# Transposing each normalized row block once in the first pass of a split-precision Strassen product

## The chip, the cores and the metric

The kernel runs on one core of a Trainium2 chip, in one launch. The metric is the device time of the program in microseconds (us). Of the kernel before the change, three runs gave 2653.09, 2655.56 and 2656.48 us, a median of 2655.56.

## The reference, cut to what matters

Two layers work on x of 2048 rows by 1024. The change lies in the first layer's first product, h @ w_in:

```python
h = rms_norm(x, a_norm_g)            # x * rsqrt(mean(x*x) + 1e-6) * g
u, v, z = split(h @ w_in, 3)         # w_in: 1024 x 6144
u = gelu(u)
v = layer_norm(gelu(v), a_ln_g, a_ln_b)
mixed = W_s applied to v in groups of 128 rows, + b_s
x = x + (u * mixed * silu(z)) @ w_out
```

The second layer (chunked band attention and its products) follows and is not touched.

## The kernel before

All data are float32. A float32 factor is split into a high and a low part (type fp32r), and a product is made of three matmuls, high by high, high by low and low by high (`mm3`, lines L111 to L113). The high part is a cast on ACT (L434), the low part a subtraction on DVE (L437), both in `split`.

The product h @ w_in is done by Strassen's scheme. h is cut into 16 row blocks of 128; pair j (0 to 7) is made of block 2j, held in the tile `ha` j, and block 2j+1, held in `hb` j. Each block has two halves of 512 columns: a11, a12 in `ha`, b1, b2 in `hb`. Seven combinations of these four halves are the stationary factors, called S_1 to S_7: S_1 = a11, S_2 = a12, S_4 = b2, S_5 = b1 + b2, S_6 = S_5 - a11, S_7 = a11 - b1 (kept in the tile `h21`), S_3 = a12 - S_6. The additions and subtractions are made by POOL: L734 (h21), L735 (b1 += b2), L736 (a11 becomes S_6), L753 (a12 becomes S_3). The weights are combined likewise: `rw` is a raw weight tile, `ch` a sum of such tiles (POOL, L445), and `T` the split factor.

The columns of w_in are cut into passes n = 0 to 5. A pass has seven phases in the order 1, 2, 6, 5, 7, 4, 3 (`PH`), each with a step for each of the eight pairs. In the phases 1 and 2 of n = 0, a step serves the pass n = 1 too and has two products; every other step has one. A product is twelve matmuls into one PSUM bank (tag "mm", four banks), which is evicted by ACT in phase 1 (L574) and by DVE elsewhere (L570); c, x and y are the accumulators.

A factor must have the inner dimension on the partitions, so each combination is transposed on PE, four 128 x 128 transposes (L611) into a PSUM tile `t0` of one bank (tag "t0", four banks). `s_split` does this in the pass n = 0: it transposes, splits into a tile S (six buffers), and one step later stores the tile to DRAM (`hsd`, L614, on SP's queue, ordered behind the latest eviction by `paced`). Every later use loads it from `hsd` (L602).

`run_steps` writes the program's order: at step s first the list `events[s]`, then the products and evictions of the step, then `prep` of step s + 3, which makes or loads that step's S, then the list `ts[s]`. `prep0` is the `prep` of n = 0: it makes S_1, S_2, S_6 and S_3 and loads the others. S_4, S_5 and S_7 are made ahead: `block_c` makes S_4 and issues the three POOL operations, `block_d` makes S_5, and S_7 is made in phase 5.

`block_norm` returns the four functions that normalize a block: the load of x (L697, SP), the Square with row sums (L703, ACT), the power -0.5 (L709 on DVE, L710 on POOL), the scaling by the row factor and g (L714, DVE). `norm_at` puts them into `ts` and `events`; blocks 0 and 2 (the pairs 0 and 1) are normalized before the first step. A scheduler then orders the instructions of each engine, so an engine's order need not be the order written.

Of the kernel before, what the change touches and what calls it, by code (L numbers as in the profile page):

```python
# [9 lines left out]
F32 = mybir.dt.float32  # L10
# [7 lines left out]
P = 128  # L18
S = 2048
# [14 lines left out]
def trunk_kernel(  # L34
# [19 lines left out]
    nc = tc.nc  # L54
# [26 lines left out]
    ident = cst.tile([P, P], F32, name="ident")  # L81
# [26 lines left out]
    mm, tpose = nc.tensor.matmul, nc.tensor.transpose  # L108
# [46 lines left out]
    def block(t, b):  # L155
        xt = xf[t, b]
        half = [
            banks[0].tile([P, 4, P], F32, tag="t4", name=f"tr_b{t}_{b}_{h}", bufs=4)
            for h in range(2)
        ]  # L160
        for k in range(KD):
            ins = tpose(half[k // 4][:, k % 4, :], xt[:, k * P : (k + 1) * P], ident[:])
            if k == 0:
                on_tick(ins)
        x3 = xt[:].rearrange("p (k c) -> p k c", k=KD)
        for h in range(2):
            ks = slice(h * 4, h * 4 + 4)
            nc.scalar.copy(x3[:, ks, :], half[h][:])
        nc.sync.dma_start(xtd[t][:, b, :], xt[:])
# [214 lines left out]
    with ExitStack() as actx:  # L384
# [26 lines left out]
        def s_tile(name):  # L411
            return ca.tile([P, 2, 4, P], F32R, tag="S", name=name, bufs=6)
# [10 lines left out]
        def in_order(key, ins):  # L423
            if key in last:
                behind(ins, last[key])
            last[key] = ins.ins.name

        def paced(ins):

            if "evict" in last:  # L430
                behind(ins, last["evict"])

        def split(hi, lo, src, key=None):
            ins = nc.scalar.copy(hi, src)  # L434
            if key:
                in_order(key, ins)
            nc.vector.tensor_tensor(lo, src, hi.bitcast(F32), op=sub)  # L437
            return ins
# [158 lines left out]
        def s_views(t):  # L597
            return [(t[:, 0, k, :], t[:, 1, k, :]) for k in range(4)]

        def s_load(ph, j, n):  # L600
            t = s_tile(f"S{n}_{ph}_{j}")
            nc.sync.dma_start(  # L602
                t[:].rearrange("p a k c -> p a (k c)").bitcast(F32), hsd[ph, j][:]
            )
            return s_views(t)

        def s_split(ph, j, rows):

            pt = ptp[0].tile([P, 4, P], F32, tag="t0", name=f"t0_{ph}_{j}", bufs=4)
            for k in range(4):  # L610
                tpose(pt[:, k, :], rows[:, k * P : k * P + P], ident[:])  # L611
            t = s_tile(f"S0_{ph}_{j}")
            split(t[:, 0], t[:, 1], pt[:], "S")
            later(1, lambda: paced(nc.sync.dma_start(  # L614
                hsd[ph, j][:], t[:].rearrange("p a k c -> p a (k c)").bitcast(F32)
            )))
            return s_views(t)
# [5 lines left out]
        def later(steps, f_):  # L623
            late.append((now[0] + steps, f_))
# [62 lines left out]
        ptp = [ptx.enter_context(tc.tile_pool(name="pt0", bufs=1, space=PSUM))]  # L687
        gab = p0.tile([P, D], F32, name="gab")
        ha = {}
        h21 = {}  # L690

        def block_norm(blk, t):

            r = sm.tile([P, 1], F32, tag="rr", name=f"ra{blk}", bufs=4)

            def load():
                nc.sync.dma_start(t, x[blk * P : (blk + 1) * P, :])  # L697
                if blk == 0:
                    nc.sync.dma_start(gab[:], a_norm_g.partition_broadcast(P))

            def square():
                jk = ca.tile([P, D], BF16, tag="acc", name=f"jk{blk}", bufs=25)
                ins = nc.scalar.activation(  # L703
                    jk[:], t, AF.Square, scale=1.0 / 32, accum_out=r[:]
                )
                last["square"] = ins.ins.name

            def power():
                nc.vector.tensor_scalar(r[:], r[:], EPS, None, op0=add)  # L709
                ins = nc.gpsimd.tensor_tensor(r[:], r[:], mhalf[:], op=ALU.pow)  # L710
                last["power"] = ins.ins.name

            def scale():
                nc.vector.scalar_tensor_tensor(t, t, r[:], gab[:], op0=mul, op1=mul)  # L714

            return load, square, power, scale

        def block_a(j):
            h = ha[j] = p0.tile([P, D], F32, tag="ha", name=f"ha{j}", bufs=8)
# [3 lines left out]

        def block_b(j):
            h = hb[j] = p0.tile([P, D], F32, tag="hb", name=f"hb{j}", bufs=3)
            return block_norm(2 * j + 1, h[:])

        def block_c(j):

            h = hb[j]  # L730
            s3 = h21[j] = p0.tile([P, 512], F32, tag="h21", name=f"h21_{j}", bufs=8)
            a11, b1_, b2_ = ha[j][:, 0:512], h[:, 0:512], h[:, 512:1024]
            s_split(4, j, b2_)
            behind(nc.gpsimd.tensor_tensor(s3[:], a11, b1_, op=sub), last["power"])  # L734
            nc.gpsimd.tensor_tensor(b1_, b1_, b2_, op=add)  # L735
            nc.gpsimd.tensor_tensor(a11, b1_, a11, op=sub)  # L736
# [7 lines left out]
        def prep0(ph, j):  # L744
            a11, a12 = ha[j][:, 0:512], ha[j][:, 512:1024]
            if ph == 1:
                return s_split(1, j, a11)
            if ph == 2:
                return s_split(2, j, a12)
            if ph == 6:  # L750
                return s_split(6, j, a11)
            if ph == 3:
                nc.gpsimd.tensor_tensor(a12, a12, a11, op=sub)  # L753
                return s_split(3, j, a12)
            return s_load(ph, j, 0)
# [131 lines left out]
        ts = {}  # L887
        events = {}

        def at(s, f_):  # L890
            events.setdefault(s, []).append(f_)

        for n in range(6):
            for ph in PH:
                where = in_t(n, ph)
                s = start.get((n, ph), start[0, ph])
# [18 lines left out]
        def norm_at(load, s, block, j):  # L915
            todo = []

            def first():
                todo.extend(block(j))
                todo.pop(0)()  # L920

            ts.setdefault(load, []).append(first)
            at(s, lambda: todo.pop(0)())
            ts.setdefault(s, []).append(lambda: todo.pop(0)())
            at(s + 1, lambda: todo.pop(0)())

        def first_two():
            for fs in zip(block_a(0), block_a(1)):
                for f_ in fs:
                    f_()  # L930
# [7 lines left out]
        ])  # L938
        at(1, lambda: nc.scalar.mul(bsh[:], bsh[:], 0.5))
        for j in range(NJ):  # L940
            e = j * 7 // 4
            norm_at(e - 1, e, block_b, j)
            at(e + 2, lambda j=j: block_c(j))
            at(e + 4, lambda j=j: block_d(j))
            at(start[0, 5] + j, lambda j=j: s_split(7, j, h21[j]))
# [12 lines left out]
        for n in range(2, 6):  # L958
# [3 lines left out]
            for r, offs in ((0, (5, 9, 13, 17)), (1, (22, 25, 28, 31))):  # L962
                for q, o in enumerate(offs):
# [4 lines left out]
                    if r == 0:  # L968
                        for i in range(2):
                            j = 2 * q + i  # L970
# [308 lines left out]
    with ExitStack() as bctx:  # L1279
# [613 lines left out]
        for t in range(NT):  # L1893
            for p in range(NPAIR):
# [3 lines left out]
                todo = []  # L1898
                if t + 1 == NT and p + 1 == NPAIR:
                    o_early[t - 1, 3] = o_right(t - 1)(3)  # L1900
                    todo = last_open()
                if t == 1 and p < 4:
                    todo = o_sums(p, lambda n: half_tile("C", n, 4), lambda n: half_tile(
                        "S", n, 4, F32R
                    ))
# [90 lines left out]
```

## Time and profile before

| | before |
| --- | --- |
| median of three runs | 2655.56 us |
| span of the profiled execution | 2652.0 us |
| around the span (median less span) | 3.56 us |
| mean granted clock of PE | 0.996 |
| ACT copy x<-P, 128 x 512 (L574) | 596 ns |
| DVE low part S<-t,S, 128 x 512 (L437) | median 682 ns |

No time is given for the profiled execution by itself; its span is 2652.0 us. In a row of the timeline, the first number is the start in us, the second the length in us, and the bracket holds the idle time before it with what ended it. In a row of a group the numbers are the busy time in us and the mean ns of one, then the engine's idle time before these instructions with its releaser. `T<-rw,T` means output T, inputs rw and T; buffer numbers are left out. PE is the matmul unit, PEld its weight loads, PEclk the clock that it was granted. SPq is SP's queue: a DMA instruction there ends when it is issued, not when its data lands.

### The profile page before, as it was taken

How to read it: one execution, taken by the hardware profiler on the slowest of the kernel's cores; microseconds unless marked ns; L12 is line 12 of the kernel's file. 1: busy time of each engine (PE TensorE's matmuls, PEld its weight loads, DVE VectorE, ACT ScalarE, POOL GpSimd, SP SyncE). 2: the span in 40 equal slices, each digit the busy share in tenths (PEclk: the TensorE clock that was granted, in tenths of full speed). 3: DMA queues.
4: the chain of work that ended last, by engine and by line, in shares of the span. 5: the costliest groups of instructions: out<-in, count | busy, mean ns of one | idle time of the engine just before them, and what ended most of it. 6: DMA issues, size and time to landing. Idle time of an engine off the chain costs nothing. (4 is left out here: it accounts for less than half of the span.)

```text
span 2652.0 us, 37980 instructions
## 1 busy us (share of the span) xinstructions
PE 2608.0 (98%) x12960; PEld 2181.4 (82%) x12960; DVE 1885.1 (71%) x2944; ACT 1303.2 (49%) x2303; POOL 897.2 (34%) x874
## 2 busy tenths in 40 slices
PE   8999999999999999999989999999999999999997
PEld 7888888888888888888878878888888888888886
DVE  5655676865767667757767767777778777877677
ACT  5422243442533434343356456666666655666564
POOL 3611334142152322203234434344332232332245
PEclk9999999999999999999999999999999999999999
DMA  7898998989989869967776597778787666875667
GB/s 286 313 344 329 346 370 323 323 323 338 330 302 313 308 233 324 331 206 270 280 251 214 186 280 229 231 245 263 252 270 254 226 204 224 255 230 161 195 224 251
DMA packets 273856, 718.72 MB, mean 271 GB/s; under 512 B 28800, under 2 KB 68736, under 8 KB 273664
## 3 DMA queue, kind: packets, MB, share of 16 engines
q1 hardware_dynamic: 273664, 716.31, 78.4%
q8 instruction: 103, 1.69, 0.3%
q14 instruction: 89, 0.73, 0.1%
HBM read 531.12 MB, written 174.59 MB: 266 GB/s over the span
## 5 line engine op out<-in xcount | busy, mean ns | idle before, releaser
L111 PE MATMUL P<-T,S 128*128 128x512 f32 x1248 | 496.2, 398 | 2.1 <-ACT S L434 2.1
L112 PE MATMUL P<-T,S 128*128 128x512 f32 x1248 | 488.2, 391 | 1.1 <-DVE T L437 1.1
L113 PE MATMUL P<-T,S 128*128 128x512 f32 x1248 | 488.6, 391 | 0.0
L1417 POOL TENSOR_SCALAR pr<-pr,sl 128x640 f32<-128x640 f32 (+4 forms) x256 | 209.7, 819 | 530.4 <-DVE sl L1416 445.2
L111 PE MATMUL pj<-hh_b,wh_b 128*128 128x512 f32 x768 | 320.4, 417 | 0.0
L113 PE MATMUL pj<-hh_b,wl_b 128*128 128x512 f32 x768 | 305.0, 397 | 1.2 <-DVE wl_b L229 1.1
L112 PE MATMUL pj<-hl_b,wh_b 128*128 128x512 f32 x768 | 303.4, 395 | 0.1
L1413 ACT ACTIVATE pr<-pr,nm 128x640 f32<-128x640 f32 (+4 forms) x256 | 195.5, 764 | 188.1 <-DVE nm L1406 186.6
L113 PEld LDWEIGHTS P<-T,S 128*128 128x128 f32 x1248 | 234.9, 188 | 50.5
L111 PEld LDWEIGHTS P<-T,S 128*128 128x128 f32 x1248 | 235.5, 189 | 46.9 <-ACT S L434 2.3
L112 PEld LDWEIGHTS P<-T,S 128*128 128x128 f32 x1248 | 235.6, 189 | 46.1 <-DVE T L437 1.3
L1438 DVE TENSOR_TENSOR pt<-tp,pt 128x640 fp32r<-128x640 f32 (+4 forms) x256 | 188.4, 736 | 43.7 <-ACT pt L1437 41.1
L1406 DVE CUSTOM_DVE_ANT_0 pr<-s,bias 128x640 f32<-128x640 f32 (+4 forms) x256 | 187.9, 734 | 35.7 <-PE s L1398 29.8
L1437 ACT CAST pt<-tp 128x640 fp32r<-128x640 f32 (+4 forms) x256 | 159.0, 621 | 54.0 <-PE tp L1433 49.8
L1433 PE MATMUL tp<-ident,pr 128*128 128x128 f32 x1120 | 166.7, 275 | 8.6 <-DVE pt L1438 7.3
L113 PEld LDWEIGHTS pj<-hh_b,wl_b 128*128 128x128 f32 x768 | 144.7, 188 | 36.4 <-DVE wl_b L229 3.8
L1433 PEld LDWEIGHTS tp<-ident,pr 128*128 128x128 f32 x1120 | 130.7, 140 | 43.3 <-issue 13.7
L111 PEld LDWEIGHTS pj<-hh_b,wh_b 128*128 128x128 f32 x768 | 145.8, 190 | 18.1 <-ACT wh_b L228 1.6
L1458 PEld LDWEIGHTS pv<-pt,V 128*128 128x128 f32 x896 | 143.3, 189 | 20.8 <-DVE pt L1438 3.9
L112 PEld LDWEIGHTS pj<-hl_b,wh_b 128*128 128x128 f32 x768 | 145.8, 190 | 17.1 <-DVE hl_b L186 0.6
L1458 PE MATMUL pv<-pt,V 128*128 128x256 f32 (+3 forms) x896 | 154.5, 320 | 2.2 <-ACT pt L1437 1.1
L229 DVE TENSOR_TENSOR wl_b<-raw_b,wh_b 128x1024 fp32r<-128x1024 f32 x96 | 120.4, 1255 | 28.5 <-ACT wh_b L228 27.8
(294 smaller groups left out, 5725.9 us busy)
## 6 DMA issues: line engine op xcount, KB each, us to landing
S<-hsd SPq DMA_DIRECT2D x288, 512.0 KB, 5.3
rw<-in_w_a SPq DMA_DIRECT2D x108, 512.0 KB, 6.3
A<-ytd SPq DMA_DIRECT2D x72, 512.0 KB, 5.7
raw_b<-wk SPq DMA_DIRECT2D x72, 512.0 KB, 4.3
hsd<-S SPq DMA_DIRECT2D x56, 512.0 KB, 4.9
V<-vhd SPq DMA_DIRECT2D x56, 512.0 KB, 5.4
bias<-reld SPq DMA_DIRECT2D x64, 320.0 KB, 4.2
va<-vd SPq DMA_DIRECT2D x32, 512.0 KB, 5.5
```

The lines of the kernel that those rows point to most:

```text
L111: first = mm(ps, lh, rh, start=first, stop=False)
L112: mm(ps, lh, rl, start=False, stop=False)
L113: mm(ps, ll, rh, start=False, stop=last)
L229: tv(wl[:], raw[:], wh[:].bitcast(F32), op=sub)
L1406: nc.vector.tensor_tensor_reduce(out=pr[:, c0:].rearrange("p (a b) -> p a b", a=nseg), in0=ps[:, :nseg, :w], in1=bias[:, c0:].rearrange("p ...
L1413: nc.scalar.activation(pr[:, c0:], pr[:, c0:], AF.Exp, scale=-1.0, bias=nm[:], accum_out=sl[:])
L1417: nc.gpsimd.tensor_scalar(pr[:, c0:], pr[:, c0:], sl[:], 1.0, op0=ALU.mult, op1=ALU.mult)
L1433: ins = tpose(tp[:, b, :], pr[:, b * P : (b + 1) * P], ident[:])
L1437: nc.scalar.copy(oh, tp[:, b0:5, :].rearrange("p a b -> p (a b)"))
L1438: nc.vector.tensor_tensor(pt[:, 2560 + o + b0 * P : 2560 + o + 640], tp[:, b0:5, :].rearrange("p a b -> p (a b)"), oh.bitcast(F32), op=ALU ...
L1458: mm(po[:, q0 * P : q1 * P], vtl[t, p][:, i, hs], rhs, start=(i == blocks[0] and j == 0), stop=(i == 7 and j == 1),)
```

## The change

The transposes leave `s_split`. `block_norm` gets a fifth function, `turn`: it transposes both halves of a normalized block, eight transposes into two PSUM tiles, which are kept in the table `turned`. `put_back` copies such a tile over the half that it came from, on ACT. From then on `ha` and `hb` hold the transposed halves, and the POOL operations and splits work on these. A B block is put back right behind its turn; an A block in `prep0` of phase 1, behind the split of S_1, which still reads the PSUM tile. All other splits read SBUF. The turn is written one step behind the block's scaling. The B blocks come at e = 2j instead of e = 7j // 4, and their loads two steps ahead of e instead of one.

```diff
         def s_split(ph, j, rows):
-            pt = ptp[0].tile([P, 4, P], F32, tag="t0", name=f"t0_{ph}_{j}", bufs=4)
-            for k in range(4):
-                tpose(pt[:, k, :], rows[:, k * P : k * P + P], ident[:])
             t = s_tile(f"S0_{ph}_{j}")
-            split(t[:, 0], t[:, 1], pt[:], "S")
+            split(t[:, 0], t[:, 1], rows.rearrange("p (k c) -> p k c", k=4), "S")
...
-            return load, square, power, scale
+            def turn():
+                for i in range(2):
+                    pt = ptp[0].tile([P, 512], F32, tag="t0", name=f"t0_{blk}_{i}", bufs=4)
+                    for k in range(4):
+                        c = slice(k * P, k * P + P)
+                        tpose(pt[:, c], t[:, i * 512 + k * P : i * 512 + k * P + P], ident[:])
+                    turned[blk, i] = pt[:]
+
+            return load, square, power, scale, turn
+
+        turned = {}
+
+        def put_back(blk, t, i):
+            nc.scalar.copy(t[:, i * 512 : i * 512 + 512], turned.pop((blk, i)))
...
         def block_b(j):
             h = hb[j] = p0.tile([P, D], F32, tag="hb", name=f"hb{j}", bufs=3)
-            return block_norm(2 * j + 1, h[:])
+            fs = block_norm(2 * j + 1, h[:])
+
+            def turn():
+                fs[-1]()
+                for i in (1, 0):
+                    put_back(2 * j + 1, h[:], i)
+
+            return *fs[:-1], turn
...
             if ph == 1:
-                return s_split(1, j, a11)
+                views = s_split(1, j, turned[2 * j, 0])
+                for i in (0, 1):
+                    put_back(2 * j, ha[j][:], i)
+                return views
...
             at(s + 1, lambda: todo.pop(0)())
+            if s < -1:
+                at(s + 1, lambda: todo.pop(0)())
+            else:
+                ts.setdefault(s + 1, []).append(lambda: todo.pop(0)())
...
         for j in range(NJ):
-            e = j * 7 // 4
-            norm_at(e - 1, e, block_b, j)
+            e = j * 2
+            norm_at(e - 2, e, block_b, j)
```

The scheduler's order moves at three places that matter below. In the names, `S0_4_1` is the S tile of pass 0, phase 4, pair 1; `hsd` and `rw` have the phase behind them too (`rw0_2_100`: pass 0, phase 2, then the tile's place), and the last number of a name only counts.

First, SP's queue in phase 1. Before:

```order
L614 DMA hsd1_3_202<-S0_1_3_517 128x1024
L614 DMA hsd1_4_203<-S0_1_4_573 128x1024
L614 DMA hsd4_0_223<-S0_4_0_589 128x1024
L470 DMA rw0_2_100_636<-in_w_a 128x1024
L697 DMA hb2_640<-in_x 128x1024
```

And after:

```order
L611 DMA hsd1_3_202<-S0_1_3_543 128x1024
L611 DMA hsd1_4_203<-S0_1_4_604 128x1024
L470 DMA rw0_2_100_682<-in_w_a 128x1024
L611 DMA hsd4_0_223<-S0_4_0_637 128x1024
L694 DMA hb2_698<-in_x 128x1024
```

The load of the first weight tile of phase 2 has moved ahead of the store of S_4 of pair 0; the load of hb2 stays behind both.

Second, DVE's order in phase 2, where hb6 is scaled. Before, it stands here:

```order
L709 TENSOR_SCALAR ra13_1056<-ra13_1056 128x1
L714 SCALAR_TENSOR_TENSOR hb6_1055<-hb6_1055,ra13_1056,gab_341 128x1024
L437 TENSOR_TENSOR S0_2_4_1052<-t0_2_4_1047,S0_2_4_1052 128x512
L437 TENSOR_TENSOR S0_4_5_1064<-t0_4_5_1059,S0_4_5_1064 128x512
L570 TENSOR_TENSOR c0_2_1091<-P0_2_2_1078,x0_2_611 128x512
```

And after:

```order
L706 TENSOR_SCALAR ra13_1145<-ra13_1145 128x1
L437 TENSOR_TENSOR S0_4_5_1215<-hb5_1032,S0_4_5_1215 128x512
L711 SCALAR_TENSOR_TENSOR hb6_1144<-hb6_1144,ra13_1145,gab_341 128x1024
L570 TENSOR_TENSOR c0_4_1245<-P0_2_4_1232,x0_4_793 128x512
L437 TENSOR_TENSOR S0_2_7_1262<-ha7_453,S0_2_7_1262 128x512
```

The scaling comes two evictions later in the phase (it stands ahead of c0_4's eviction, not c0_2's), the low part of S_4 of pair 5 stands ahead of it, and the low parts read `hb` and `ha` in SBUF where they read the PSUM tile `t0`.

Third, DVE's order near the end of phase 5, where y is evicted and S_7 is split. Before:

```order
L437 TENSOR_TENSOR S0_7_4_1746<-t0_7_4_1741,S0_7_4_1746 128x512
L570 TENSOR_TENSOR y0_4_1763<-P0_5_4_1750,x0_4_728 128x512
L437 TENSOR_TENSOR S0_7_5_1778<-t0_7_5_1773,S0_7_5_1778 128x512
L570 TENSOR_TENSOR y0_5_1795<-P0_5_5_1782,x0_5_800 128x512
L437 TENSOR_TENSOR S0_7_6_1808<-t0_7_6_1803,S0_7_6_1808 128x512
```

And after:

```order
L437 TENSOR_TENSOR S0_7_4_1713<-h21_4_1087,S0_7_4_1713 128x512
L570 TENSOR_TENSOR y0_4_1730<-P0_5_4_1717,x0_4_793 128x512
L570 TENSOR_TENSOR y0_5_1757<-P0_5_5_1744,x0_5_841 128x512
L437 TENSOR_TENSOR S0_7_5_1740<-h21_5_1214,S0_7_5_1740 128x512
L570 TENSOR_TENSOR y0_6_1782<-P0_5_6_1769,x0_6_908 128x512
```

The low part of S_7 of pair 5 now stands behind the eviction of y of pair 5. On SP's queue, before and after, the store of that S_7 stands right ahead of the load of S_7 of pair 0.

## The prediction

> **What bounds the kernel now.** I read the page first: span and busy time.
>
> ```profile
> span 2652.0 us, 37980 instructions
> PE 2608.0 (98%) x12960; PEld 2181.4 (82%) x12960; DVE 1885.1 (71%) x2944; ACT 1303.2 (49%) x2303; POOL 897.2 (34%) x874
> ```
>
> PE works 2608.0 of 2652.0 us, so time goes down where PE gets less to do, or where one of its few pauses closes. The change touches only the pass n=0. So the second view is the table of windows over it, with its bounds at the starts of phases 2, 6, 5 and 7.
>
> ```profile
> core 0: us, PE busy (x) PEld busy (x) DVE busy (x) ACT busy (x) POOL busy (x), PEclk, DMA share, GB/s
> 0.00:71.34 71.34, 62.16 (x292) 51.66 (x293) 40.92 (x51) 39.82 (x68) 27.73 (x35) 0.95 0.77 290
> 71.34:123.00 51.66, 51.66 (x265) 43.44 (x264) 35.19 (x53) 25.02 (x42) 37.46 (x29) 1.00 0.86 307
> 123.00:147.00 24.00, 24.00 (x118) 19.84 (x117) 13.29 (x20) 6.32 (x11) 7.59 (x6) 1.00 1.00 379
> 147.00:172.00 25.00, 25.00 (x127) 20.61 (x126) 13.24 (x18) 6.06 (x11) 2.57 (x2) 1.00 0.93 338
> 172.00:280.00 108.00, 108.00 (x493) 89.29 (x493) 63.36 (x88) 29.07 (x42) 21.24 (x16) 1.00 0.92 330
> ```
>
> From 71.34 on PE is busy for the whole of each window: nothing that is late on DVE, ACT, POOL or the queues reaches it, and a transpose that goes is time that goes. But the cover is thin: in phase 2 (second row) DVE and POOL are busy 35.19 and 37.46 of 51.66 us, and from 123 to 172 the DMA engines are busy for 1.00 and 0.93 of the time.
>
> The third view is the tile view of the transposes' line, and the fourth PE's timeline round three places: the start, one group of four transposes among matmuls, and the one long pause.
>
> ```profile
> L611 PE MATMUL t<-ident,ha x128: 270/272/328, 8.1 to 233.8; 128*128 128x128 f32 x128
> L611 PE MATMUL t<-ident,hb x64: 272/273/447, 28.5 to 123.0; 128*128 128x128 f32 x64
> L611 PE MATMUL t<-ident,h x32: 270/272/273, 147.3 to 170.1; 128*128 128x128 f32 x32
>   DVE hb L714: 4.0, 1
>   DVE ra L709: 0.3, 1
> ```
>
> ```profile
> 10.82 0.50 PE L111 MATMUL P<-T,S 128*128 128x512 f32 x1 [2.07 <-ACT S L434]
> 13.03 0.51 PE L112 MATMUL P<-T,S 128*128 128x512 f32 x1 [1.08 <-DVE T L437]
> ...
> 20.46 0.60 PE L611 MATMUL t<-ident,ha 128*128 128x128 f32 x4
> 20.82 0.48 PE L113 MATMUL P<-T,S 128*128 128x512 f32 x1
> 21.13 0.39 PE L111 MATMUL P<-T,S 128*128 128x512 f32 x1
> 21.36 0.40 PE L112 MATMUL P<-T,S 128*128 128x512 f32 x1
> ...
> 46.45 0.60 PE L611 MATMUL t<-ident,hb 128*128 128x128 f32 x4
> 51.10 1.09 PE L611 MATMUL t<-ident,hb 128*128 128x128 f32 x4 [4.04 <-DVE hb L714]
> 51.84 0.78 PE L111 MATMUL P<-T,S 128*128 128x512 f32 x1
> ...
> 54.50 0.40 PE L111 MATMUL P<-T,S 128*128 128x512 f32 x1
> ```
>
> **Part 1: fewer transposes.** Before, 128+64+32 = 224 transposes run, 56 groups of four; after, 16 blocks of two groups, 32. A group and the matmul behind it take from 20.46 to 21.13, 0.67 us, where a matmul alone takes 0.23 (21.13 to 21.36): a group costs 0.44. With the next weights load behind it I take 0.45. At the start PE waits 2.07 and 1.08 us in any case: two groups are hidden there now, and four after, since both halves of pairs 0 and 1 are turned there. So 54 visible groups become 28: 26 x 0.45 = **-11.7 us**. Some 21 of the 26 lie behind 123, in phases 6, 5 and 3.
>
> **Part 2: the pause at 47 us.** The next rows are SP's and ACT's of that place.
>
> ```profile
> 18.26 21.59 SPq L614 DMA_DIRECT2D hsd<-S  x6
> 39.90 0.42 SPq L470 DMA_DIRECT2D rw<-in_w_a  x1
> ```
>
> ```profile
> 45.43 1.05 ACT L434 CAST T<-rw 128x1024 fp32r<-128x1024 f32 x1 [10.35 <-DMA rw<-in_w_a]
> ```
>
> SP issued six stores from 18.26 to 39.85; the sixth, hsd4_0, waited for DVE. The load of the first weights of phase 2 stood behind them and went out at 39.90. ACT's cast of it waited 10.35 us, and behind the cast stood hb2's Square: so hb2 was scaled late and PE stood for 4.04 us. Then the clock was down: the group at 51.10 took 0.74 instead of 0.36 to the next start, and six matmuls took 2.66 (51.84 to 54.50) instead of 6 x 0.23 = 1.38. That is 4.04 + 0.38 + 1.28 = 5.7, and with the small pause of 0.3 before, 6.0. After, this load stands ahead of hsd4_0 (first order piece), behind stores that wait for casts of phase 1 alone. I take the whole: **-6.0 us**; the other end is 0, since hb2's own load still stands behind hsd4_0.
>
> **Part 3: more copies on ACT.** 32 copies of a PSUM tile come new. The nearest row is the eviction copy of phase 1, of the same shape:
>
> ```profile
> L574 ACT COPY x<-P 128x512 f32<-128x512 f32 x16 | 8.8, 596 | 7.9 <-PE P L113 7.9
> ```
>
> 32 x 0.6 = 19 us on an engine that idles half of the time, mostly beside PE. One place shows: hb0's Square now stands behind eight more copies, 8 x 0.6 = 4.8 us, and PE's turn of hb0 waits for it, by my walk along the queues about 1.15 us near 29 us. **+1.15**, between 0 and 4.8.
>
> The sum so far: 2652.0 - 11.7 - 6.0 + 1.15 = 2635.45 of span. What lies around the span is 2655.56 - 2652.0 = 3.56, by the median, as no time is given for the profiled execution by itself. That makes **2639.0**.
>
> **Part 4: S lows that read SBUF twice.** Of the 56 subtractions that make the low half of an S tile, 48 now read their rows from SBUF, not PSUM. Their own length does not change:
>
> ```profile
> L437 DVE TENSOR_TENSOR So<-A,So x64: 672/686/1779, 1070.8 to 1293.0; 128x512 fp32r<-128x512 f32 x64
> L437 DVE TENSOR_TENSOR S<-t,S x56: 675/682/693, 11.2 to 234.8; 128x512 fp32r<-128x512 f32 x56
> L437 DVE TENSOR_TENSOR T<-rw,T x42: 1207/1224/2328, 11.8 to 941.4; 128x1024 fp32r<-128x1024 f32 x42
> ```
>
> The form with one PSUM input never leaves 0.69; the two forms with two SBUF inputs have maxima 1.09 and 1.10 us above their medians. The timeline shows what those meet (POOL's rows first, then DVE's):
>
> ```profile
> 74.45 1.29 POOL L734 TENSOR_TENSOR h<-ha,hb 128x512 f32<-128x512 f32 x1
> 75.82 2.15 POOL L735 TENSOR_TENSOR hb<-hb 128x512 f32<-128x512 f32 x1
> ...
> 79.29 1.29 POOL L734 TENSOR_TENSOR h<-ha,hb 128x512 f32<-128x512 f32 x1
> 80.66 1.30 POOL L735 TENSOR_TENSOR hb<-hb 128x512 f32<-128x512 f32 x1
> ```
>
> ```profile
> 74.52 2.30 DVE L714 SCALAR_TENSOR_TENSOR hb<-hb,ra,gab 128x1024 f32<-128x1024 f32 x1 [0.66 <-POOL ra L710]
> ...
> 108.01 1.29 DVE L714 SCALAR_TENSOR_TENSOR hb<-hb,ra,gab 128x1024 f32<-128x1024 f32 x1 [0.67 <-POOL ra L710]
> ...
> 79.31 1.87 DVE L437 TENSOR_TENSOR S<-t,S 128x512 fp32r<-128x512 f32 x3
> ```
>
> The scale, two SBUF inputs, takes 2.30 beside a POOL subtraction and 1.29 alone; the POOL operation behind it takes 2.15 instead of 1.29. Three S lows from PSUM beside POOL take 1.87 and lengthen nothing. So the two engines take turns, an operation at a time, and the 48 lows join the queue.
>
> This is where a rule speaks against the change. The Trainium skill, page "SBUF — State Buffer", section "Who interferes with whom", says that a DVE instruction with two SBUF inputs contends with a GpSimd instruction that reads SBUF, that whichever comes first keeps the shared port for its whole length, and that one with a single SBUF input does not contend. The rows agree with it (2.30 against 1.29; 1.87 for three).
>
> What it costs: in phase 2, in the new order of DVE and POOL, some 14 S lows (9.5 us), three scales and four T lows (8.7) exclude about 35 us of POOL's work (the window's 37.46 less some 2.5 by which waits stretch it), 53 in all. The phase holds 16 products of twelve matmuls, so (265 - 192) / 4 = 18 groups of transposes now and 10 after: it would last 51.66 - 8 x 0.45 = 48.1, and 5 us are too much. Charging each wait along the queues, I find PE paused before the turn of hb6 (its scale stands behind POOL; second order piece), at four evictions and before S_6_3, together about 10; if POOL's early subtractions for phase 3, which nobody waits for yet, take the delay, it is 0. I take **+5**, the overflow, which lies between the two.
>
> **Part 5: loads that come later.** Behind 123 DMA is at its limit and PE shall run faster: the two windows move 379 x 24.00 + 338 x 25.00 = 17.5 MB, in 43.2 us after 13 groups less, 406 GB/s where 379 is the highest here. At 379 it takes 46.3: 3.1 more. And S_7_0's load:
>
> ```profile
> 165.73 0.38 SPq L602 DMA_DIRECT2D S<-hsd  x1
> ```
>
> ```profile
> S<-hsd SPq DMA_DIRECT2D x16, 512.0 KB, 5.7
> ```
>
> The second row is the median landing between 130 and 180 us, 5.7. The load went out at 165.73; it is needed twelve matmuls behind the last transposes of h (170.1 + 12 x 0.23 = 172.9), 7.2 later: 1.5 to spare. After, its store hsd7_5 waits for the S_7_5 low, which now stands behind y_5's eviction on DVE (third order piece): it is issued two phase-5 steps ahead of the need, less some 2 us for the eviction, the low (0.69 each) and the store's issue: 2 x 2.76 - 2 = 3.5, so it comes 2.2 late, and the next load again in part. Both together **+3.5**, from 0 to 7.
>
> Weights of phases 7, 4 and 3 move 14 to 34 places down SP and stay in time by my walk. The B blocks come every two steps instead of every 1.75, and their loads go out two steps ahead instead of one: the work of hb7 moves by two steps to the end of phase 2, which the ten above contains. Forecast: 2639.0 + 5 + 3.5 = **2647.5**.
>
> **The rivals.** One more row, from DVE's waits between 71.34 and 172:
>
> ```profile
> DVE hb L714 <- POOL ra L710: 7.7, 3, 6.3
> ```
>
> *Full gain:* turns between DVE and POOL and later loads fall into slack, 2639 to 2643. For it: DVE waited 7.7 us for POOL, 6.3 at one time, and PE had no pause from it. Against: the 53 us of turns. Chance 0.20. *The gain is used up:* 10 for part 4 and 7 for part 5 give 2656, or the pause of part 2 stays: 2654.5. Near no change, 2651 to 2660, chance 0.31. *Slower, by turn-taking:* each of some 30 S lows from S_4_0 to S_6_3 meets a POOL operation that has just begun, and waits 1.29. That is 38.7 us, of which DVE's idle time in phase 2 takes 51.66 - 35.19 = 16.5: 22.2 of pauses, with part 5 2639.0 + 22.2 + 3.5 = 2664.7. It is slower once the mean wait passes (16.5 + 16.6 + 5.3 - 3.5) / 30 = 1.16. For it: maxima of 1.09 to 1.10. Against: those are maxima, medians are at the bare length. Chance 0.11. By the Trainium skill's rule, taken at its worst, it is this case. *No gain, as transposes were covered:* PE busy 51.66 of 51.66 leaves 0.01.
>
> **How the numbers follow.** The likeliest case, 2643 to 2651, has 0.37. A measurement here tells 0.2%, 5.3 us, from no change: faster is below 2650.25, slower above 2660.9. Faster gets 0.20 and most of the likeliest, 0.56; same the rest of it and the used-up case, 0.32; slower 0.12. The range runs from the full gain, 2638, to 2659, and leaves out the slower case and the ends.
>
> **What would show it.** Right: 32 groups of transposes; no pause of 4 us near 47; phase 2 starting about 3 us earlier; S lows from ha and hb at up to 1.8 us beside POOL, and POOL's rows at up to 2.2; pauses of PE before hb6's turn and at S_7_0. Wrong: S lows at 0.69 throughout and no new pause (full gain), a pause above 3 us in phase 1, or DVE idle below 10% in phase 2 with PE waiting for evictions (slower).

## The result, and the profile after

The change makes the kernel slower by a little, where a gain was forecast. Over 19 runs of each kernel, beside each other, the changed kernel takes 2664.51 us (2657.82 to 2669.25) and the kernel before 2656.48 (2650.98 to 2662.33). The ratio is 1.0030, with a 95% interval of 1.0024 to 1.0037: 8 us more. The forecast was 2647.5, with a range from 2638 to 2659, and the result lies outside it. The profiled execution of the changed kernel is one of its faster ones, 2658.81 us by its own time and 2657.0 by its span; its mean granted clock is 0.998, that of the median run 0.995. So 1.8 us lie around a span, not the 3.56 of the prediction, and the profile of before with its span of 2652.0 stands for about 2653.8.

First the page of the changed kernel, span and busy time.

```profile
span 2657.0 us, 37825 instructions
PE 2597.1 (98%) x12864; PEld 2168.0 (82%) x12864; DVE 1894.7 (71%) x2944; ACT 1318.4 (50%) x2335; POOL 899.4 (34%) x874
```

PE is busy for 10.9 us less than before (2608.0), and yet the span is 5.0 longer: PE now waits. The windows of the changed kernel, with the same bounds as those of before (the columns are the same), say where.

```profile
0.00:71.34 71.34, 66.21 (x338) 55.54 (x339) 41.27 (x50) 53.13 (x95) 28.55 (x34) 1.00 0.79 288
71.34:123.00 51.66, 46.34 (x214) 38.15 (x213) 39.72 (x48) 24.07 (x42) 34.11 (x27) 0.97 0.76 274
123.00:147.00 24.00, 21.29 (x91) 16.51 (x90) 20.36 (x26) 10.04 (x17) 10.08 (x7) 1.00 1.02 366
147.00:172.00 25.00, 22.12 (x96) 17.39 (x95) 11.27 (x16) 5.64 (x9) 2.52 (x2) 1.00 0.92 324
172.00:280.00 108.00, 102.09 (x448) 83.40 (x447) 65.01 (x90) 29.57 (x43) 25.93 (x19) 1.00 0.93 341
```

In the first window PE gained, 66.21 busy us against 62.16. In the other four, where it had no idle time before, it idles for 5.3, 2.7, 2.9 and 5.9 us. Here are PE's pauses between 60 and 400 us, from its timeline; the bracket holds the length and what ended it. The kernel before has none in this stretch.

```profile
106.02 1.94 PE L718 MATMUL t<-ident,hb 128*128 128x128 f32 x8 [4.11 <-DVE hb L711]
121.75 0.47 PE L111 MATMUL P<-T,S 128*128 128x512 f32 x1 [1.22 <-DVE c L570]
128.14 0.47 PE L111 MATMUL P<-T,S 128*128 128x512 f32 x1 [0.53 <-DVE c L570]
131.48 0.50 PE L111 MATMUL P<-T,S 128*128 128x512 f32 x1 [0.36 <-ACT S L434]
134.03 0.50 PE L113 MATMUL P<-T,S 128*128 128x512 f32 x1 [1.82 <-DVE S L437]
148.94 0.47 PE L111 MATMUL P<-T,S 128*128 128x512 f32 x1 [1.46 <-DVE x L570]
166.23 0.47 PE L111 MATMUL P<-T,S 128*128 128x512 f32 x1 [0.69 <-DMA S<-hsd]
169.96 0.47 PE L111 MATMUL P<-T,S 128*128 128x512 f32 x1 [0.72 <-DVE y L570]
178.15 0.50 PE L111 MATMUL P<-T,S 128*128 128x512 f32 x1 [2.47 <-DMA S<-hsd]
219.11 0.47 PE L111 MATMUL P<-T,S 128*128 128x512 f32 x1 [2.57 <-DMA S<-hsd]
244.87 0.47 PE L111 MATMUL P<-T,S 128*128 128x512 f32 x1 [0.87 <-DVE vst L634]
...
329.13 0.47 PE L111 MATMUL P<-T,S 128*128 128x512 f32 x1 [2.38 <-DMA S<-hsd]
```

The reader is to see two groups. Up to 134 us the pauses are ended by DVE and ACT; behind 148 mostly by a load of S. The last of them, at 329, lies in phase 4 of the pass n = 1, a pass whose code the diff does not touch. Taken from start to start of PE's instructions, with the slow matmuls behind a pause (below), the first group costs 10.9 us and the second 12.3, together 23.2. The forecast had 5 + 3.5 for all of them. The gain of the first three parts was to be 16.6: 23.2 - 16.6 = 6.6 us slower. Evictions at 400 us come 5.8 later than before, the distance stays near that up to 1000 us, and at the end the two spans differ by 5.0.

The S lows in the changed kernel, grouped by their inputs within the first 285 us (busy us, mean ns):

```profile
L437 DVE TENSOR_TENSOR S<-ha,S 128x512 fp32r<-128x512 f32 x24 | 20.6, 883 | 0.0
L437 DVE TENSOR_TENSOR S<-hb,S 128x512 fp32r<-128x512 f32 x16 | 17.4, 1090 | 2.7 <-ACT S L434 2.7
L437 DVE TENSOR_TENSOR S<-h,S 128x512 fp32r<-128x512 f32 x8 | 5.5, 683 | 0.0
```

Beside POOL they are longer, by 0.20 us for `ha` and 0.41 for `hb` against the 0.683 of those that meet no POOL work (`h`, in phase 5): 24 x 0.20 + 16 x 0.41 = 11.4 us, a mean of 0.28 for each of the 40.

### The profile page after: what moved, and what is told of

It is laid out like the page before. It is cut to its first block, busy times and chain, and to the rows that moved or that the text cites. A ratio compares the mean times of both kernels' runs of the same rounds, so it can differ in the third digit from the quotient of the medians.

```text
span 2657.0 us, 37825 instructions
## 1 busy us (share of the span) xinstructions
PE 2597.1 (98%) x12864; PEld 2168.0 (82%) x12864; DVE 1894.7 (71%) x2944; ACT 1318.4 (50%) x2335; POOL 899.4 (34%) x874
```

## The experiments

The theories after the result. **L (turn-taking):** S lows that read SBUF twice and POOL's operations take turns, and PE waits for what comes late by that. **Q (queue order):** a few instructions stand in the wrong place of an in-order queue, behind something that waits. **D (the DMA limit):** from phase 6 on the DMA engines are full, so a PE that runs ahead waits for its loads. Each kernel was timed beside the kernel before; on its scale 0.001 is 2.7 us, and the changed kernel is at 1.0030.

| run | edit | median, us | ratio, 95% interval |
| --- | --- | --- | --- |
| e1 | power ahead of a weights' combination | 2660.84 | 1.0007, 0.9997 to 1.0017 |
| e2 | S_7 split two steps earlier | 2662.09 | 1.0020, 1.0011 to 1.0028 |
| e3 | S lows with one SBUF input | 2656.62 | 0.9999, 0.9990 to 1.0009 |
| e4 | before, without transposes of S_7, S_3 | 2652.40 | 0.9988, 0.9978 to 0.9998 |
| e5 | S_3 subtractions later | 2662.14 | 1.0020, 1.0009 to 1.0032 |
| e6 | S_7 split at its use | 2651.12 | 0.9983, 0.9974 to 0.9992 |
| e7 | before, weights of phase 2 earlier | 2654.20 | 0.9993, 0.9984 to 1.0002 |
| e8 | five repairs together | 2642.74 | 0.9953, 0.9941 to 0.9964 |
| e9 | e6 with 4 MB of other copies | 2659.56 | 1.0014, 1.0005 to 1.0022 |
| e10 | e1 and e6 | 2646.34 | 0.9968, 0.9958 to 0.9978 |
| e11 | spacing of the B blocks undone | 2662.35 | 1.0025, 1.0015 to 1.0034 |
| e12 | e3 and e6 | 2643.49 | 0.9957, 0.9943 to 0.9970 |

**e1.** The edit to the changed kernel:

```diff
             at(s, lambda: todo.pop(0)())
-            ts.setdefault(s, []).append(lambda: todo.pop(0)())
+            at(s, lambda: todo.pop(0)())
...
-                    v = comb(chain[n](q), raw(1, 1), t1)
+                    v = comb(chain[n](q), raw(1, 1), t1, after=None if n else last["power"])
```

(`comb` orders its two POOL operations behind the instruction given.) Expected:

> The changed kernel, with the power of a B block's row sums set on POOL ahead of the second combination of weights for phase 6 (ch <- rw, ch), and written ahead of the step's product instead of behind it. Theory Q (queue order): the 4.11 us pause of PE before hb6's turn, and the slow clock behind it (1.6 us), come from that power standing on POOL behind a combination that waits for its weights; both go, so the kernel comes out 4 to 6 us below the changed one, at 0.999 to 1.001 of the kernel before. Theory L (turn-taking of DVE and POOL because S lows read SBUF twice): hb6's scale is late through the lock, so the pause stays at 3 us or more and the ratio at 1.003.

In the changed kernel POOL's timeline before the pause at 106 reads:

```profile
99.30 2.54 POOL L445 TENSOR_TENSOR ch<-rw,ch 128x512 f32<-128x512 f32 x2 [2.50 <-DMA rw<-in_w_a]
101.80 1.26 POOL L751 TENSOR_TENSOR h<-ha,hb 128x512 f32<-128x512 f32 x1
103.02 0.55 POOL L707 TENSOR_TENSOR ra<-ra,mhalf 128x1 f32<-128x1 f32 x1
```

The power that hb6's scale needs, 0.55 us of work, stands behind a combination that itself waited 2.50 us for its weights. DVE answered to it:

```profile
103.60 2.27 DVE L711 SCALAR_TENSOR_TENSOR hb<-hb,ra,gab 128x1024 f32<-128x1024 f32 x1 [4.76 <-POOL ra L707]
```

In e1 the power runs at 97.05, ahead of that combination, and the pause before hb6's turn is gone:

```profile
97.05 0.56 POOL L709 TENSOR_TENSOR ra<-ra,mhalf 128x1 f32<-128x1 f32 x1
98.64 3.14 POOL L445 TENSOR_TENSOR ch<-rw,ch 128x512 f32<-128x512 f32 x2 [1.04 <-DMA rw<-in_w_a]
```

```profile
107.54 0.50 PE L111 MATMUL P<-T_hl,S 128*128 128x512 f32 x1 [2.08 <-DVE c L572]
```

A smaller pause comes in its place, for an eviction on DVE, and eight matmuls behind it are still slow, by 1.7 us in all. From start to start the pauses and slow matmuls between 100 and 135 us fall from 10.9 to 7.9, 3 us less. The ratio falls by 0.0023, 6 us, so the one profile shows half of what the medians do. Theory Q holds for the pause before hb6's turn, not for the slow matmuls.

**e5 and e11** try the same place in other ways. e5 orders POOL's S_3 subtractions behind the last POOL operation of pair 7:

```diff
-            nc.gpsimd.tensor_tensor(a11, b1_, a11, op=sub)
+            last["s6"] = nc.gpsimd.tensor_tensor(a11, b1_, a11, op=sub).ins.name
...
-                nc.gpsimd.tensor_tensor(a12, a12, a11, op=sub)
+                behind(nc.gpsimd.tensor_tensor(a12, a12, a11, op=sub), last["s6"])
```

> The changed kernel, with POOL's eight subtractions for S_3 (a12 minus S_6, 8 x 1.6 us, needed only in phase 3) ordered behind the last POOL operation of pair 7 instead of among the work of phase 2. Nothing is left out. Theory L (turn-taking): some 10 us of POOL's work leave the stretch where S lows and POOL take turns; S lows from ha and hb drop from a mean of 0.88 and 1.09 us towards 0.75 and 0.9, the pauses of PE between 100 and 135 us (11.7 us in all) fall by 4 us or more, and the ratio goes to 1.001 to 1.002. Theory Q (queue order alone): the power of hb6 still stands behind the weights' combination, the 4.11 us pause and its 1.6 us of slow clock stay, and the sum falls by less than 3 us.

The pause at 105 is 3.16 us, with slow matmuls behind it for another 1.7, and the sum between 100 and 135 us falls from 10.9 to 8.9: 2 less, as theory Q had it. The ratio, 1.0020, is what theory L had, but its interval overlaps that of the changed kernel. The S lows from `ha` become longer (939 ns for 883) and those from `hb` shorter (958 for 1090): the subtractions, moved, meet the lows of phase 6. This run does not tell L from Q. e11 undoes the spacing:

```diff
-            e = j * 2
-            norm_at(e - 2, e, block_b, j)
+            e = j * 7 // 4
+            norm_at(e - 1, e, block_b, j)
```

> The changed kernel with the B blocks at e = 7j // 4 again and their loads one step ahead (that part of the change undone). Theory Q: hb6's power stands ahead of the waiting weights' combination on POOL, so the 4.11 us pause and its slow clock go, 4 to 6 us in all, ratio 1.001 to 1.002; new pauses of up to 3 us may come in phase 1, where the B blocks are turned earlier. If the spacing does not matter, the ratio stays at 1.003.

Here theory Q, in the form that blamed the spacing, was wrong. The pause stays, and is longer, now before the turn of hb7:

```profile
110.31 1.94 PE L718 MATMUL t<-ident,hb 128*128 128x128 f32 x8 [5.26 <-DVE hb L711]
```

```profile
105.86 2.48 POOL L445 TENSOR_TENSOR ch<-rw,ch 128x512 f32<-128x512 f32 x2
108.31 0.54 POOL L707 TENSOR_TENSOR ra<-ra,mhalf 128x1 f32<-128x1 f32 x1
```

```profile
108.88 1.28 DVE L711 SCALAR_TENSOR_TENSOR hb<-hb,ra,gab 128x1024 f32<-128x1024 f32 x1 [2.86 <-POOL ra L707]
```

hb7 was loaded late (SP issued its load at 95.75, the Square ran at 103.08), and once more the power stood behind a combination: DVE was idle for 2.86 us until it came. So POOL's queue accounts for some 2.9 of the 5.26 us, and under either spacing a power stands behind a combination; the rest is the late load.

**e3 and e12** take the second SBUF input away:

```diff
-            split(t[:, 0], t[:, 1], rows.rearrange("p (k c) -> p k c", k=4), "S")
+            src = rows.rearrange("p (k c) -> p k c", k=4)
+            if ph == 1:
+                split(t[:, 0], t[:, 1], src, "S")
+            else:
+                in_order("S", nc.scalar.copy(t[:, 0], src))
+                nc.vector.tensor_tensor(t[:, 1], src, zp[:].rearrange("p (k c) -> p k c", k=4), op=sub)
```

(`zp` is a PSUM tile of zeros; three banks are left for `t0`.)

> The changed kernel, but the 48 S lows from SBUF subtract a PSUM tile of zeros instead of the high part, so each reads SBUF once (the low part's value is left out; one PSUM bank of the transposes goes to the zeros, three are left). Theory L: S lows go back to 0.69 us each, POOL's subtractions to 1.29, and most of the 11.7 us of pauses before phase 5 go: 7 us or more below the changed kernel, ratio 1.000 or less. Theory Q: lengths go back in the same way, but the pause before hb6's turn stays at 3 us or more, and the kernel gains 2 to 4 us, ratio 1.0015 to 1.0025.

The groups of e3 show the S lows at their bare length:

```profile
L615 DVE TENSOR_TENSOR S<-ha,zp 128x512 fp32r<-128x512 f32 x24 | 15.9, 677 | 1.3 <-DMA hsd<-S 1.0 <-PE P L113 0.3
L615 DVE TENSOR_TENSOR S<-hb,zp 128x512 fp32r<-128x512 f32 x16 | 10.8, 676 | 4.1 <-ACT hb L733 4.1
```

Between 50 and 138 us PE has no pause of note left, and the time falls by 0.0031, 8.2 us. So the first group of pauses hangs on what e3 takes away, hb6's pause among them, as theory L had it. That is the second input, and one thing more: the low part no longer reads the high part, so it does not wait for ACT's cast either. e3 does not part the two, but in the groups of the changed kernel the wait for that cast is 2.7 us and the lengthening 11.4. The gain of e3 at hb6's turn and that of e1 are not two separate ones: the power still stands behind the combination in e3, but it runs at 99.53 instead of 103.02 and PE, delayed by a pause of 1.65 at 46 us for a PSUM bank, asks for hb6 at 103.87 instead of 101.9. What e3 gains is then met by a new pause, at the start of phase 5, and by the loads behind it, 12 us in all from 138 on, and 3 more of slow matmuls:

```profile
142.76 0.76 PE L111 MATMUL P<-T,S 128*128 128x512 f32 x1 [3.88 <-DMA S<-hsd]
```

**e2 and e6** go at the second group. e2 moves the split of S_7 only in time:

```diff
-            at(start[0, 5] + j, lambda j=j: s_split(7, j, h21[j]))
+            at(start[0, 5] + j - 2, lambda j=j: s_split(7, j, h21[j]))
```

> The changed kernel, with the split of S_7 two steps earlier, so that its store no longer stands behind the eviction of y on DVE. Theory Q: PE's pauses at 165, 169 and 175 us (0.85 + 0.88 + 2.63 = 4.4 us) come from loads of S that go out late on SP; they go, and the ratio to the kernel before falls from 1.003 to about 1.0015. Rival D (the DMA engines are at their limit in phases 6 and 5): the same bytes still have to pass, pauses of 3 us or more in all stay somewhere between 120 and 200 us, and the ratio stays at 1.0025 or more.

The ratio is 1.0020, between the two expectations. The load of S_7 is no longer late, but the pauses move: five between 151 and 171 us, 4.8 us in all, each ended by a load, the longest being

```profile
171.07 0.47 PE L111 MATMUL P<-T,S 128*128 128x512 f32 x1 [2.44 <-DMA S<-hsd]
```

and only the one near 219 shrinks, to 0.66. Behind the pause at 171 and behind the one near 329 the matmuls are slow, by 1.7 us each, so that the second group costs as much as in the changed kernel. Theory D comes closer than Q. e6 saves the loads instead:

```diff
-            at(start[0, 5] + j, lambda j=j: s_split(7, j, h21[j]))
...
                 return s_split(3, j, a12)
+            if ph == 7:
+                return s_split(7, j, h21[j])
```

> The changed kernel, with S_7 split from h21 in the step's preparation in phase 7, as S_6 and S_3 are, and not in phase 5: eight loads of 512 KB from hsd are gone, and the eight stores of S_7 move from phase 5 to phase 7. Nothing is left out. Rival D (the DMA engines are at their limit): the pauses that end with a load of S between 145 and 200 us (0.7 + 2.5, with 0.8 after an eviction) go, 4 us in all, and the ratio falls to about 1.0015; the pause near 219 us, at a load of S_4, shrinks too. Theory Q: the pauses of phase 5 and 7 go as well, since the late load is gone, but the one near 219 stays at 2 us or more; DVE, which now has a split in each step of phase 7 beside two evictions, could pause PE there instead.

It gains three times what was expected, 0.0047 or 12.5 us. Its pauses up to 149 us are those of the changed kernel; behind 149 there is none at all up to 400, where the changed kernel has six with 10.7 us from start to start. The window row of e6 for that stretch:

```profile
200.00:335.00 135.00, 135.00 (x597) 111.83 (x596) 82.98 (x123) 36.80 (x53) 30.64 (x21) 1.00 0.92 336
```

The pauses at 219 and 329 went too, and e6 leaves those places alone. SP's order tells how: in the changed kernel the load of S_4_7 stands behind four weight loads, which wait for free buffers, and the loads of S1_4_6 and S1_4_7 (pass n = 1) behind weights that wait until sums of w_out are stored. SP's timeline of the changed kernel, for the first place:

```profile
203.18 9.15 SPq L470 DMA_DIRECT2D rw<-in_w_a  x4
212.38 0.42 SPq L635 DMA_DIRECT2D vd<-x  x1
212.86 0.42 SPq L602 DMA_DIRECT2D S<-hsd  x1
```

The kernel before has four weight loads in this place too, but there they are through in 3.7 us:

```profile
198.01 0.48 SPq L470 DMA_DIRECT2D rw<-in_w_a  x1
...
199.24 0.45 SPq L470 DMA_DIRECT2D rw<-in_w_a  x1
...
200.52 1.17 SPq L470 DMA_DIRECT2D rw<-in_w_a  x2
...
203.46 0.33 SPq L602 DMA_DIRECT2D S<-hsd  x1
```

So at 219 the wait is new and not the order; in n = 1 the order is new, since before both weight loads stand ahead of three of the stores. In e6 the scheduler has the four out ahead of the first load of phase 4, and in n = 1 both weight loads ahead of three of the four stores. Between 145 and 200 us the DMA engines of e6 move no less than those of the changed kernel, 18.82 MB against 18.66 (14 loads of S in place of 20, 9 of weights in place of 3). So it is not the sum of bytes in this stretch that makes PE wait there.

**e9** asks whether it is the bytes:

```diff
             if ph == 7:
+                nc.sync.dma_start(spare[j][:], hsd[1, j][:])
                 return s_split(7, j, h21[j])
```

> The kernel of e6 (S_7 split at its use), with eight copies of 512 KB from DRAM to DRAM put where the eight loads of S_7 were; nobody waits for their data. They tell whether e6 gained by the bytes or by the loads that PE no longer waits for. Bytes (rival D): pauses of PE before loads of S come back between 145 and 330 us, 5 us or more in all, and the ratio goes from 0.9983 back to 1.000 or more. Late loads: the pauses stay away and the ratio stays within 0.001 of 0.9983.

The ratio goes from 0.9983 to 1.0014, two thirds of the way back, and three pauses stand between 145 and 335 us, 8.0 us from start to start, each with slow matmuls behind it for another 1.7. The first, at 151, is in the place where e6 has 1.49 for an eviction; the two largest are

```profile
218.74 0.47 PE L111 MATMUL P<-T,S 128*128 128x512 f32 x1 [2.97 <-DVE vst L634]
...
329.22 0.75 PE L111 MATMUL P<-T,S 128*128 128x512 f32 x1 [2.51 <-DMA S<-hsd]
```

though nobody waits for these copies. Some 2 us of the delay stand ahead of the first copy, which goes out at 159: hb6's turn runs at 107.86 instead of 105.92. And the scheduler also sets S_4_7 and S1_4_6 behind the weights again when the copies are there, so bytes and order come back together, and these runs do not part them.

**e4 and e7** price the gains from the side of the kernel before. e4 leaves 16 groups of transposes out:

```diff
-            pt = ptp[0].tile([P, 4, P], F32, tag="t0", name=f"t0_{ph}_{j}", bufs=4)
-            for k in range(4):
-                tpose(pt[:, k, :], rows[:, k * P : k * P + P], ident[:])
+            if ph in (7, 3):
+                pt = rows.rearrange("p (k c) -> p k c", k=4)
+            else:
+                pt = ptp[0].tile([P, 4, P], F32, tag="t0", name=f"t0_{ph}_{j}", bufs=4)
+                for k in range(4):
+                    tpose(pt[:, k, :], rows[:, k * P : k * P + P], ident[:])
...
```

> The kernel before, with the transposes of S_7 and S_3 left out (these two split the rows as they are, so that part of the transposing is not done): 16 groups of four fewer, in phases where POOL is nearly idle. Taken at 0.45 us each the kernel gains 7.2 us, ratio 0.9973, if transposes on PE are time and nothing else moves. If the loads of S behind them come too late (theory Q) or the DMA engines are at their limit (rival D), PE shows new pauses in phases 5 to 4 and the gain is under 4 us.

By the evictions, phase 5 gains 3.9 us over its eight steps (from 0.5 us later than before to 3.4 earlier), 0.49 a group, and after phase 3 of n = 0 they come 7.2 earlier: the price of the prediction, 0.45, is near. Then 2.5 us are given back far from the edit, in phase 4 of n = 1,

```profile
318.95 0.47 PE L111 MATMUL P<-T,S 128*128 128x512 f32 x1 [2.23 <-DMA S<-hsd]
```

and the measured gain is 3.2 us. e7 takes the part of the prediction on the pause at 47 us by itself:

```diff
-                    offs = ((-6, 1), (-5, 1), (-4, 1))
+                    offs = ((-7 if ph == 2 else -6, 1), (-5, 1), (-4, 1))
```

> The kernel before, with the first weights of phase 2 of n = 0 loaded one step earlier, so that this load stands ahead of the stores hsd1_4 and hsd4_0 on SP. One part of the change alone (its side effect on SP's order). If the pause of 4.04 us near 47 us hangs on that load, as the prediction said, it goes with the slow clock behind it: 5.7 us, ratio 0.9979. If hb2's own load is the limit, a pause of 2 us or more stays and the ratio is 0.999 or more.

The pause shrinks from 4.04 to 3.02, and the gain is 1.9 us, with an interval that reaches 1.0002:

```profile
50.49 0.63 PE L611 MATMUL t<-ident,hb 128*128 128x128 f32 x4 [3.02 <-DVE hb L714]
```

hb2's own load goes out at 40.79 there, 0.42 later than before, and its Square waits for it until 47.05. The pause stays above 2 us, as the second branch of the expectation has it. But the load is not the limit alone: ACT's cast ahead of the Square waited for the next weights and ended only 0.29 us earlier.

**e8, e10 and e12** put repairs together. e10 has the edits of e1 and e6, e12 those of e3 and e6. e8 has the edits of e1, e5 and e6, and these:

```diff
+                s_split(4, j, turned[2 * j + 1, 1])
                 for i in (1, 0):
                     put_back(2 * j + 1, h[:], i)
...
-            s_split(4, j, b2_)
...
-            for f_, o in zip(out_sums(q), (-3, 0, 2)):
+            for f_, o in zip(out_sums(q), (-5, -2, 0)):
```

> The changed kernel with the repairs of e1 (the power ahead of the weights' combination) and e6 (S_7 split at its use) alone. If the two causes are separate, their gains add: 1.003 - 0.0023 - 0.0047 = 0.996. If the earlier start of phase 6 only meets the DMA limit sooner, as e3 did, the gain of e1 is lost and the ratio stays near 0.998.

The gains nearly add: 0.9968 (0.9958 to 0.9978), where 0.996 was the sum. The pauses left are DVE's in phases 2 and 6, but for 0.35 at a cast of ACT and 0.56 at a load of S near 339.

> The changed kernel with five repairs: the power ahead of the weights' combination on POOL, the S_3 subtractions behind pair 7's, S_4 split straight from the PSUM tile of the turn (eight S lows fewer that read SBUF twice), S_7 split at its use, and the sums of w_out two steps earlier (so that the loads of S in phase 4 of n = 1 do not stand behind weights that wait for buffers). Nothing is left out. If the pauses found in the trace are the cause of the loss, 23 us of pauses fall to 8 or less and the kernel comes out at 0.996 to 0.998 of the kernel before. If DMA sets the time of phases 6 to 4 whatever the order, 10 us or more of pauses stay and the ratio is 0.999 or more.

e8 is faster than both kernels: 2642.74 us, 0.9953 of the kernel before. Its pauses between 60 and 400 us are these and one of 0.44 at a load of S:

```profile
121.67 0.47 PE L111 MATMUL P<-T,S 128*128 128x512 f32 x1 [0.49 <-DVE c L572]
125.63 0.50 PE L111 MATMUL P<-T,S 128*128 128x512 f32 x1 [0.96 <-ACT S L434]
127.62 0.79 PE L113 MATMUL P<-T,S 128*128 128x512 f32 x1 [1.26 <-DVE S L437]
```

> The kernel of e3 (S lows with one SBUF input; the low part's value is left out) with S_7 split at its use as in e6. With both the turn-taking and the loads of phase 7 gone, what is left is the sum of the prediction's first three parts: -11.7 - 6.0 + 1.15 = -16.6 us, ratio 0.9938. If the gain of fewer transposes is smaller than 0.45 us each, or phase 5 still waits for its first loads (3.9 us in e3), the ratio is 0.9955 or more.

e12 comes to 0.9957 (0.9943 to 0.9970), with 0.9938 just outside. One pause of size stands where e3 has it, for phase 5's first loads:

```profile
141.85 0.58 PE L111 MATMUL P<-T,S 128*128 128x512 f32 x1 [3.33 <-DMA S<-hsd]
```

Its span is 2640.9. Less that pause from start to start (3.5) and the slow matmuls behind it (1.7), one of 0.6 in n = 1, and the 0.8 by which its pauses in phase 1 exceed the 1.15 of the prediction, 2634.3 remain, where parts 1 to 3 gave 2635.45. This is one profile, and the sum is an estimate from its rows.

## Why the prediction was wrong, point by point

**What bounds the kernel** was right: PE, with thin cover. The warning that phases 6 and 5 are at the DMA engines' limit stood in it, and was given too small a price.

**Part 1, fewer transposes:** right. The groups are 32, and one costs 0.49 (e4) against 0.45.

**Part 2, the pause at 47 us:** right in its result, in part by luck. The pause is gone, and the load of the weights goes out at 26.48 instead of 39.90. But e7 shows that this load by itself is worth about a quarter of the pause; what was left hung on hb2's own load, the other end that the prediction named, and on the next weights. In the changed kernel hb2's load is hardly earlier (39.44 instead of 40.37), and its scale ends at 48.90 instead of 50.95. A turn at 47, where PE stood ready before, would still have waited 1.9 us. But PE asks for hb2 later, its turn runs at 54.66. So about half of the pause goes because hb2 is ready earlier, and a later turn, which the part did not count on, covers the rest.

**Part 3, copies on ACT:** right, 1.05 us at 29.41 where 1.15 was said.

**Part 4, S lows that read SBUF twice:** the step that sized it failed, 10.9 us instead of 5, and just above the upper end of 10. The mechanism was right in kind (e3). The overflow was worked out from busy time alone, 53 us of turns in 48, as if both engines could fill every gap. The walk that gave 10 came closer, because it followed the order: it named hb6's turn, evictions and S_6, and the trace has its pauses at hb6's turn, at two evictions and at two S tiles. What the part does not name is that POOL, ahead of hb6's power, itself waits 2.50 us for weights, and that slow matmuls follow: 4.11 us of pause there and 1.6 behind it. The rule of the Trainium skill (page "SBUF — State Buffer", section "Who interferes with whom") that was cited there agrees with the trace in kind: S lows of one shape run from 669 to 1785 ns. What it costs in time follows from the queues, not from the rule.

**Part 5, later loads:** the step that failed by most, 12.3 us instead of 3.5, and beyond its upper end of 7. The late load that it named made no pause. S_7_0's load goes out at 167.27, behind hsd7_5 as forecast, and is there when PE comes to it near 172.9. The pause of 2.47 belongs to the load behind it, S_7_1's, which goes out at 173.31 behind hsd7_6. That store was late by way of ACT: the casts of S_7_6 and S_7_7 stood behind a cast of weights that waited for POOL.

```profile
169.97 1.05 ACT L434 CAST T<-rw 128x1024 fp32r<-128x1024 f32 x1 [6.49 <-POOL rw L445]
170.92 1.13 ACT L434 CAST S<-h 128x512 fp32r<-128x512 f32 x2
```

Two things were missing from the price. It was taken as one late load and a rate, where each S load has its place in SP's one queue behind stores and weights that wait. And nothing was charged behind the phases that the diff touches, where the pauses at 219, 244 and 329 take 6.3 us: at 219 four weight loads wait for 9.15 us instead of 3.7, and at 329 the scheduler changed SP's order. The cause of the pause at 244 was not looked for. Phase 4 of n = 1 lost 2.4 to 2.5 us even in e4, with a different edit. The 379 GB/s that the part took for the highest rate is not one either (last section).

**Around the span:** 3.56 was too much; it is 1.8.

**The slower rival** gave 2664.7 us and the measured median is 2664.51, but it was not what happened. It needed a mean wait of 1.16 us or more for each S low; the trace has 0.28. The kernel got there by the loads of part 5, which the rival took at 3.5. Nearest in its sizes was the rival that the gain is used up, with 10 for part 4 and 7 for part 5; even it had 5.3 too little for the second.

**What stays open:** whether the pauses behind 149 us are due to the eight loads themselves or to the order on SP, and the waits in it, that come with them; no run has the one without the other. Also the profile of the changed kernel is 5.7 us under its median of 2664.51. The lower clock of the median run points to more slow matmuls there, but no trace of that run was kept.

## What to carry to other kernels

When an engine without idle time gets less to do, price what feeds it before booking the gain: here 16.6 us were taken off PE's path, and 23 came back as waits. Dropping one set of loads and moving one small instruction (e10) turned 8 us of loss into 8.5 of gain. A small operation on an in-order queue (the power, 0.55 us) costs what stands ahead of it, so look for what it can be put behind. And where a scheduler sets the order, compare its order in the stages behind the edit too, since this change set loads behind waiting ones 150 us later.

## What the runs showed of the hardware

In the changed kernel the DMA engines moved 402 GB/s between 130 and 140 us and 383 in the ten us after it, at busy shares of 1.03 and 1.02; in the kernel before it was 418 between 140 and 150. These are loads and stores mixed, so 379, which part 5 took for the highest rate, is not the limit over ten us.

PE's clock after a pause: behind the 4.11 us the eight transposes and three matmuls that follow take 1.6 us more than their usual time, from start to start, as behind the 4.04 before; the clock granted between 105 and 110 us is 0.66. Behind a single pause of 2.57 (at 219.11) nothing is lost. The Trainium skill, page "TensorE: Matmul & The Clock Gate", section "Part 1: The HAM clock gate (the "warmup" mystery)", puts the idle window behind which the clock is halved at about 3.4 us. Not all pauses here agree with that. In e9 the matmuls behind a pause of 2.00 us, with no other in the 15 us ahead of it, are slow, and the clock granted between 150 and 156 us is 0.72:

```profile
151.32 0.47 PE L111 MATMUL P<-T,S 128*128 128x512 f32 x1 [2.00 <-DMA S<-hsd]
151.63 0.52 PE L112 MATMUL P<-T,S 128*128 128x512 f32 x1
151.94 0.63 PE L113 MATMUL P<-T,S 128*128 128x512 f32 x1
```

In e8 the matmul at 127.62 takes 0.79 instead of 0.39 behind pauses of 0.49, 0.96 and 1.26 within 6 us, while behind a single pause of 2.78 (e11, at 328.03) none is slow. In the traces kept, up to 400 us, each pause of 2.97 us or more has slow matmuls behind it. Below that the length alone does not tell. What is lost, where it happens, is 1.4 to 1.7 us.
